# Items of 512 weight columns, taken in quarters of the contraction, in the first stage of a hybrid decoder block

## The chip, the core and the metric

The kernel runs on one core of a Trainium2 chip. The core has a matrix engine (TensorE, PE in the profile; its weight loads, which overlap, are listed as PEld), a vector engine (VectorE, DVE), an engine for activations and copies (ScalarE, ACT), a general engine (GpSimd, POOL), an engine that here only issues transfers (SyncE, SP), and 16 DMA engines. The engines run their own instruction queues in order and wait for one another by semaphores. The metric is the device time of one execution in microseconds; before the change the median of three runs is 1727.08 us (1726.94 to 1728.37).

## What is computed

One layer of a decoder block on 1024 tokens of 1024 features, all in float32. The part that matters here is the combined input projection and what takes its columns:

```
h = rms_norm(x, attn_norm_w)
proj = h @ w_in                       # columns: q 1024 | k 1024 | v 1024 | u 2048 | g 2048
q, k, v, u, g = split(proj)
q, k = rms_norm of each 64 columns of q and of k      # 8 heads of 2 x 64
a = diff_attention(q, k, v, lam, rel_bias)            # needs a bias row per head and distance
c = causal_depthwise_conv(u_a * sigmoid(u_b))         # width 31, over tokens
...
x = x + (sigmoid(g_a) * y_a + sigmoid(g_b) * y_b) @ w_out
x = x + (silu(h2 @ w_gate) * (h2 @ w_up)) @ w_down
```

## The kernel before

**Matrix products.** A float32 operand is split into a high part (a cast on ACT, `split_hi`, L120) and a low part (a subtraction, `split_lo` on DVE, L125, or `low` on POOL, L131, which of the two is set by `low_by_pool`). `mm3` (L168 to L170) issues three matmuls for a product: high by high, high by low, low by high. The normalized input stands in SBUF as `hT_hi` and `hT_lo`, 8 tiles of the contraction by 1024 tokens.

**The weight stream.** `Stream` holds a list of loads. `fetch` runs loads until more than `ahead` are ready; `next` hands out the oldest. A load takes a raw tile of 128 x 1024 (`wraw`, two buffers), issues the DMA on SP's queue, and splits it into `whi` and `wlo` (three buffers each, `wsplit`). `ld_wide` serves an item of 256 weight columns in two loads, each with half of the contraction (4 tiles of 128 rows by 256 columns).

**The first stage.** `opening` normalizes and transposes x, does V0 (v's first 256 columns) and half of U0. Then come the items of `first`, V1 and V2, each 256 columns of v; then seven u pairs (`u_pair`), which use seven products in place of eight and need sums of h (`sums_of_h`, on POOL) and of weights (`prepare`); then the items of `last`, Q0 (128 columns of q and 128 of k of the first head) and V3. After that the attention begins, with Q1 to Q7 and the g items as filling work between its steps.

`v_item` computes two token tiles of 128 x 256 into one PSUM bank (`gemm_N`: all 8 tiles of the contraction for one token tile, then the next), splits the bank into high and low, and sends both to DRAM by SP; it yields after each bank, four times. `q_item` does the same for the token half b = 1 and then b = 0, two banks each: ACT copies the bank and takes eight sums of squares, and after the second bank DVE forms 16 row factors and multiplies. The turning of q and k (`turn_qk`: transposes on PE, a scaled copy on ACT, the remainder on DVE, moves between partition halves by SP's DMAs) is put off by one yield through the list `late`.

**Banks.** In the first stage matrix products rotate over four PSUM banks (`pg`: two of tag pg, two of tag pg2). In the attention two are left, and the four banks of the convolution's accumulator and of pg2 serve the scores.

**Order.** The instructions are written in program order by these generators, and a scheduler then orders each engine's queue. At each yield of the first stage `bg.step` puts 3.25 steps of the depthwise convolution (taps on DVE, L594) into the program. `bg.until` after Q0 puts in all that is left for the first four channel tiles, whose accumulators lie in PSUM. At yields 18, 19 and 20 `bias_rows` makes a third of the bias rows: one-hot rows in and bias rows out by POOL's DMA queue, a matmul (L771) and a copy on ACT (L772) between.

Of the kernel before, what the change touches and what calls it, by code (L numbers as in the profile page):

```python
# [10 lines left out]
F32 = mybir.dt.float32  # L11
F32R = mybir.dt.float32r
AF = mybir.ActivationFunctionType
ALU = mybir.AluOpType
# [43 lines left out]
def kernel(  # L58
# [193 lines left out]
    def pcol(key, k=0):  # L252
        c = col[key] + k
        return pvec[:, c : c + 1]
# [63 lines left out]
    def ld_wide(w, cols):  # L318


        def half(g):
            def go():
                raw = wraw()
                r3 = raw[:].rearrange("p (k c) -> p k c", c=256)
                o = 0
                for c0, n in cols:
                    nc.sync.dma_start(
                        r3[:, :, o : o + n],
                        w[512 * g : 512 * (g + 1), c0 : c0 + n].rearrange(
                            "(k p) c -> p k c", p=P  # L330
                        ),
                    )
                    o += n
                hi, lo = wsplit(raw)
                return (
                    hi[:].rearrange("p (k c) -> p k c", c=256),
                    lo[:].rearrange("p (k c) -> p k c", c=256),
                )

            return go  # L340

        return [half(0), half(1)]

    class Stream:


# [52 lines left out]

    first = ["V1", "V2"]
    last = ["Q0", "V3"]
    later = [
        ["Q1", "G0", "G1"],
        ["Q2", "G2", "G3"],
# [21 lines left out]
    for c in range(NKT):  # L428
        ws.plan(ld_cols(wpa, c * P))
    for c in range(NKT):  # L430
# [331 lines left out]
    def bias_rows(c0):  # L762

        if c0 == 0:
            pool.memset(rb[:], -BIG)
            pool.dma_start(rb[:NB, :], rel_bias)
            dve.tensor_scalar(rb[:], rb[:], -1.0, None, op0=ALU.mult)
        oh, gr = half("u3")[: NB + 1, :384], half("u2")[:H, :384]
        pool.dma_start(oh, buckets[:, c0 : c0 + 384])
        o = pm()  # L770
        pe.matmul(o[:H, :384], rb[:], oh, start=True, stop=True)  # L771
        act.copy(gr, o[:H, :384])  # L772
        pool.dma_start(b_d[:, c0 : c0 + 384], gr)

    def bias_skew(h):
        pool.dma_start(t_d[h][:], b_d[h : h + 1, :].to_broadcast([P, TL]))
# [6 lines left out]
    T = {}  # L783
    late = []

    def q_item(h):
        halves = [ws.next(), ws.next()]
        t = {}
        T[h] = t
        for b in (1, 0):  # L790
            raw = qkp.tile([P, 4, 256], F32, tag="qkraw", name=nm("qkraw"), bufs=2)
            ss = sm.tile([P, 16], F32, tag="ss16", name=nm("ss16"))
            for i2 in range(2):
                o = pg()
                for e in range(2):
                    gemm_N(o[:, 256 * e : 256 * (e + 1)], halves, hT_hi, hT_lo, 4 * b + 2 * i2 + e)
                act.copy(raw[:, 2 * i2 : 2 * i2 + 2, :], o[:].rearrange("p (e c) -> p e c", c=256))
                jk = sm.tile([P, VD], F32, tag="jk", name=nm("jk"), bufs=1)[:, :HD]
                for g in range(8):
                    act.activation(  # L800
                        jk, o[:, g * HD : (g + 1) * HD], AF.Square, accum_out=ss[:, 8 * i2 + g : 8 * i2 + g + 1]
                    )
                if i2 == 0:
                    yield
            r = rstd_of(ss[:], 16, 1.0 / HD, fast=h > 0)
            r4 = raw[:].rearrange("p i (g d) -> p (i g) d", d=HD)
            dve.tensor_tensor(r4, r4, r.unsqueeze(2).to_broadcast([P, 16, HD]), op=ALU.mult)

            def turn_qk(z, key, b, raw):


                dma = nc.sync.dma_start
                pt = pm("pQ")
                for i in range(4):
                    pe.transpose(pt[:, i * P : (i + 1) * P], raw[:, i, z * P : (z + 1) * P], ident[:])  # L815
                w = pcol(key + "n")

                def part(j):
                    return qkp.tile([P, 512], F32R, tag=f"{key}s{j}", name=f"{key}s{j}_{h}_{b}", bufs=2 if key == "q" else 3)

                s1, s2 = part(1), part(2)
                act.activation(s1[:], pt[:], AF.Identity, scale=w)
                lo = part(3) if key == "q" else qkp.tile([P, 512], F32R, tag="klo", name=f"klo_{h}_{b}", bufs=1)
                dve.scalar_tensor_tensor(lo[:], pt[:], w, f32(s1[:]), op0=ALU.mult, op1=ALU.subtract)
                if key == "q":
                    dma(f32(s2[HD:, :]), f32(s1[HD:, :]))
                    lo2 = part(4)
                    for one, two in ((s1, s2), (lo, lo2)):
                        if one is lo:
                            dma(f32(two[HD:, :]), f32(one[HD:, :]))  # L830
                        dma(f32(two[:HD, :]), f32(one[HD:, :]))
                        dma(f32(one[HD:, :]), f32(one[:HD, :]))
                    t["q", b] = (s1, lo), (s2, lo2)
                else:
                    act.activation(s2[HD:, :], pt[HD:, :], AF.Identity, scale=w[HD:, :])
                    dma(f32(s2[:HD, :]), f32(lo[HD:, :]))
                    dma(f32(s1[HD:, :]), f32(lo[:HD, :]))
                    t["k", b] = s1, s2

            for z, key in ((1, "k"), (0, "q")):
                free = NT * (h - 1) + (0 if key == "k" and b else NT if key == "q" and not b else NT // 2)
                late.append((free if h else 0, lambda a_=(z, key, b, raw): turn_qk(*a_)))
            yield

    inatt = [False]
    MAKE = {"V": v_item, "U": u_item, "Q": q_item, "G": g_item}

    def run(items):  # L850
        for it in items:
# [177 lines left out]
    def first_stage():  # L1029


        nonlocal qkp
        tsum = sums_of_h()
        yield from opening()
        ups = [prepare(win, (U0 + D + c * P, U0 + c * P), st[0], 2, c == 1) for c in range(1, NKT)]

        def weights_ahead():
            yield
            ws.ahead = 1
            ws.fetch()  # L1040
# [36 lines left out]
        bg.until((NKT - CONV_PSUM) * (CW + 1) - 1)  # L1077
        yield from run(last[1:])

    def opening():  # L1080

# [1053 lines left out]
```

## Time and profile before

| what | value |
|---|---|
| median of three runs (lowest, highest) | 1727.08 us (1726.94, 1728.37) |
| profiled execution: span from its first to its last instruction | 1725.7 us |
| V1 and V2 | 65.3 to 112.0 us of the span |
| seven u pairs | 112.0 to 250.7 us |
| Q0 and V3 | 250.7 to 297.5 us |
| first scores of the attention | 306.8 us |

The profiled execution has only its span on record; the median of the runs is 1.4 us longer, which is what lies around the span. In the rows of the profile L12 is line 12 of the kernel, `out<-in` are the tiles written and read, `x3` a count, and what stands in brackets or behind a second bar is the time that the engine was idle just before and what ended it. A matmul's duration overlaps that of the next; the distance of two starts is what the engine needs for one.

### The profile page before, as it was taken

To read this page: it belongs to the slowest core of one execution; us is meant where nothing else is said; L and a number is where in the kernel's file an instruction comes from. 1 tells how busy PE (TensorE), PEld (TensorE's weight loads), DVE (VectorE), ACT (ScalarE), POOL (GpSimd) and SP (SyncE) were. 2 spreads that over 40 slices of the span, in tenths; PEclk is the share of its full clock that TensorE was granted. 3 is DMA by queue.
4 is the path that set the end of the run, shared out by engine and by line. 5 is a ranking of instruction groups with operands and counts; after the bars stand their busy time and mean duration, and the time that the engine had idled before them with its cause. 6 is when DMAs were issued, how large, how long until landed. Compare 5 with 4: busy or idle time off the path is not lost.

```text
span 1725.7 us, 25863 instructions
## 1 busy us (share of the span) xinstructions
PE 1714.6 (99%) x9243; PEld 1477.9 (86%) x9243; DVE 1275.4 (74%) x2128; ACT 862.5 (50%) x1958; POOL 219.1 (13%) x207
## 2 busy tenths in 40 slices
PE   9999999999999999999999999999999999999999
PEld 7997889998998998988788888888888888888887
DVE  7675889898988888878687769966676666575544
ACT  5333335767777776756556325633333333333332
POOL 3997851000000000000000000000000000000000
PEclk9999999999999999999999999999999999999999
DMA  6344445336345344343973683245455445598663
GB/s 208 116 126 132 131 151 154 104 109 171 104 127 147 115 125 138 101 136 130 333 238 118 200 296 119 74 135 164 147 170 170 154 141 164 175 355 285 217 215 130
DMA packets 261604, 281.64 MB, mean 163 GB/s; under 512 B 16546, under 2 KB 181986, under 8 KB 261475
## 3 DMA queue, kind: packets, MB, share of 16 engines
q1 hardware_dynamic: 254160, 267.71, 48.3%
q0 software_dynamic: 5680, 9.39, 2.6%
q10 hardware_dynamic: 1634, 2.89, 0.5%
q8 instruction: 73, 1.20, 0.3%
q14 instruction: 57, 0.46, 0.1%
HBM read 181.84 MB, written 85.50 MB: 155 GB/s over the span
## 4 chain that ended last, share of the span: by engine, by line
PE 92%; DMA 3%; DVE 2%; ACT 1%; issue 1%; POOL 0%; SPq 0%; DVEq 0%; POOLq 0%; ACTq 0%
PE acc L980 29%; PE acc L488 12%; PE pg L168 12%; PE pg L169 12%; PE pg L170 12%; PE wo L1850 3%; PE sc L1290 2%; PE sc L1289 2%; PE pT L1328 2%; PE pg L1106 1%; DVE acc L594 1%; PE pW L168 1%; PE pW L169 1%; PE pW L170 1%; PE pQ L815 1%
## 5 line engine op out<-in xcount | busy, mean ns | idle before, releaser
L594 DVE SCALAR_TENSOR_TENSOR acc<-u,cw,acc 128x1023 f32<-128x1023 f32 (+14 forms) x240 | 303.4, 1264 | 23.2 <-ACT acc L588 20.7
L170 PE MATMUL pg<-whi,hT_lo 128*128 128x256 f32 x704 | 200.2, 285 | 0.0
L168 PE MATMUL pg<-whi,hT_hi 128*128 128x256 f32 x704 | 199.7, 285 | 0.4 <-DVE v L125 0.4
L169 PE MATMUL pg<-wlo,hT_hi 128*128 128x256 f32 x704 | 199.5, 284 | 0.0
L125 DVE TENSOR_TENSOR wlo<-draw,whi 128x1024 fp32r<-128x1024 f32 x75 | 91.7, 1223 | 83.4 <-ACT whi L120 78.9
L120 ACT CAST whi<-draw 128x1024 fp32r<-128x1024 f32 x75 | 79.1, 1055 | 129.5 <-PE acc L488 114.3
L169 PEld LDWEIGHTS pg<-wlo,hT_hi 128*128 128x128 f32 x704 | 134.4, 191 | 1.8
L170 PEld LDWEIGHTS pg<-whi,hT_lo 128*128 128x128 f32 x704 | 134.3, 191 | 1.8
L168 PEld LDWEIGHTS pg<-whi,hT_hi 128*128 128x128 f32 x704 | 134.0, 191 | 2.1 <-DVE v L125 0.6
L120 ACT CAST whi<-wraw 128x1024 fp32r<-128x1024 f32 x90 | 94.7, 1052 | 70.6 <-PE pg L169 32.6
L488 PE MATMUL acc<-wlo,whi 128*128 128x512 f32 x308 | 119.8, 389 | 0.0
L488 PE MATMUL acc<-whi,wlo 128*128 128x512 f32 x308 | 119.8, 389 | 0.0
L1296 ACT ACTIVATE E<-E,mn 128x640 f32<-128x640 f32 (+7 forms) x128 | 99.8, 781 | 30.8 <-DVE mn L1291 29.2
L168 PE MATMUL pg<-hT_hi,whi 128*128 128x512 f32 x288 | 114.4, 397 | 0.1
L169 PE MATMUL pg<-hT_lo,whi 128*128 128x512 f32 x288 | 113.7, 395 | 0.0
L170 PE MATMUL pg<-hT_hi,wlo 128*128 128x512 f32 x288 | 113.7, 395 | 0.0
L120 ACT CAST whi<-s 128x1024 fp32r<-128x1024 f32 x54 | 56.9, 1053 | 104.9 <-PE acc L980 101.8
L125 DVE TENSOR_TENSOR wlo<-wraw,whi 128x1024 fp32r<-128x1024 f32 x75 | 93.3, 1246 | 12.6 <-ACT whi L120 12.3
L1291 DVE CUSTOM_DVE_ANT_0 E<-sc,tb 128x512 f32<-128x512 f32 (+3 forms) x128 | 74.2, 585 | 33.2 <-PE pT L1328 16.1
L980 PE MATMUL acc<-h_hi,whi 128*128 128x512 f32 x240 | 93.4, 389 | 0.0
L980 PE MATMUL acc<-h_lo,whi 128*128 128x512 f32 x240 | 93.4, 389 | 0.0
L980 PE MATMUL acc<-h_hi,wlo 128*128 128x512 f32 x240 | 90.1, 389 | 0.0
(370 smaller groups left out, 4589.7 us busy)
## 6 DMA issues: line engine op xcount, KB each, us to landing
wraw<-in_w_gate_up_dram SPq DMA_DIRECT2D x44, 512.0 KB, 4.7
wraw<-in_w_in_dram SPq DMA_DIRECT2D x38, 512.0 KB, 4.0
qs<-qs SPq DMA_DIRECT2D x96, 128.0 KB, 2.3
wd<-in_w_down_dram SPq DMA_DIRECT2D x44, 256.0 KB, 3.1
tdT<-wd SPq DMA_DIRECT2D x88, 128.0 KB, 4.8
draw<-sdS SPq DMA_DIRECT2D x44, 256.0 KB, 3.7
draw<-tdT SPq DMA_DIRECT2D x44, 256.0 KB, 3.7
wraw<-in_w_in_dram SPq DMA_DIRECT2D x32, 256.0 KB, 3.3
```

The lines of the kernel that those rows point to most:

```text
L120: act.copy(dst, src)
L125: last_lo[0] = dve.tensor_tensor(dst, src, f32(hi), op=ALU.subtract).ins
L168: pe.matmul(o, lh, rh, start=start, stop=False)
L169: pe.matmul(o, lh, rl, start=False, stop=False)
L170: last_mm[0] = pe.matmul(o, ll, rh, start=False, stop=stop).ins
L488: m = pe.matmul(o[s_][i][:], l_[:, ts], r_[:, 512:], start=start and j + y_ == 0, stop=j == n - 1 and y_ == 2, skip_group_check=not start,)
L594: dve.scalar_tensor_tensor(a_, us[c][:, : S - n], cw[:, c, t : t + 1], a_, op0=ALU.mult, op1=ALU.add)
L980: last_mm[0] = pe.matmul(o[:], a_[x_][:, k, :], b_[y_][:, k, :], start=start and k + x_ + y_ == 0, stop=k == 3 and x_ == 1, skip_group_che ...
L1289: pe.matmul(o[:, :w], qh[:, qs], k, start=True, stop=False)
L1291: dve.tensor_tensor_reduce(e[:, ks], o[:, :w], tb[:, S - nk + c0 : S - nk + c0 + w], 1.0, mn[:, j : j + 1] if c0 else 3.0e38, ALU.add, ALU ...
L1296: act.activation(e[:, :nk], e[:, :nk], AF.Exp, bias=mn[:, j : j + 1], scale=-1.0, accum_out=l[:, j : j + 1])
L1850: last_mm[0] = pe.matmul(o[s_][i][:], A[u_], B[v_], start=start and j + y_ == 0, stop=j == 3 and y_ == 2, skip_group_check=not start,).ins
```

## The change

V1 and V2 become one item W1 of 512 columns of v; Q0 and V3 become one item W0 of 512 columns (128 of q, 128 of k, 256 of v). A load (`ld_quarters`) brings a quarter of the contraction, 2 tiles of 128 rows by 512 columns, so a raw tile is as large as before. A wide item works on four token tiles at a time, each with a bank of its own: quarter 0 for all four tiles, then quarter 1, 2 and 3. The second block of four token tiles takes quarters 1, 2, 3 and then 0, which is loaded a second time.

```diff
+    def ld_quarters(w, cols):
+        def quarter(g):
+            def go():
+                raw = wraw()
+                r3 = raw[:].rearrange("p (k c) -> p k c", c=512)
+                o = 0
+                for c0, n in cols:
+                    nc.sync.dma_start(
+                        r3[:, :, o : o + n],
+                        w[256 * g : 256 * (g + 1), c0 : c0 + n].rearrange("(k p) c -> p k c", p=P),
+                    )
+                    o += n
+                hi, lo = wsplit(raw)
+                return g, [t_[:].rearrange("p (k c) -> p k c", c=512) for t_ in (hi, lo)]
+            return go
+        return [quarter(g) for g in (0, 1, 2, 3, 0)]
...
-    first = ["V1", "V2"]
-    last = ["Q0", "V3"]
+    first = ["W1"]
+    last = ["W0"]
...
+        if it[0] == "W":
+            cols = [(V0 + 256, 512)] if c else [(Q0, P), (K0, P), (V0 + 768, 256)]
+            return ld_quarters(win, cols)
...
-        pool.dma_start(oh, buckets[:, c0 : c0 + 384])
+        nc.sync.dma_start(oh, buckets[:, c0 : c0 + 384])
...
-        pool.dma_start(b_d[:, c0 : c0 + 384], gr)
+        nc.sync.dma_start(b_d[:, c0 : c0 + 384], gr)
...
+    def wide_item(c):
+        def v_parts(i, o, j, n):
+            vh, vl = [t_[:, :n] for t_ in v_tiles[0]()]
+            split_hi(vh, o)
+            split_lo(vl, o, vh)
+            for src, dst in ((vh, v_hi), (vl, v_lo)):
+                for e in range(n // 256):
+                    nc.sync.dma_start(dst[j + e][i * P : (i + 1) * P, :], f32(src[:, 256 * e : 256 * (e + 1)]))
+        w = []
+        for second, b in enumerate((0, 1) if c else (1, 0)):
+            banks = [pg() for i in range(4)]
+            if c == 0:
+                raw = qkp.tile([P, 4, 256], F32, tag="qkraw", name=nm("qkraw"), bufs=2)
+                ss = sm.tile([P, 16], F32, tag="ss16", name=nm("ss16"))
+            for n in range(4):
+                if second and n < 3:
+                    g, (hi, lo) = w[n + 1]
+                else:
+                    ws.ahead = 0 if n == 3 else 1
+                    w.append(ws.next())
+                    g, (hi, lo) = w[-1]
+                for i in range(4):
+                    ts = slice((4 * b + i) * P, (4 * b + i + 1) * P)
+                    o = banks[i]
+                    for k in range(2):
+                        mm3(
+                            o[:], hT_hi[:, 2 * g + k, ts], hT_lo[:, 2 * g + k, ts], hi[:, k, :], lo[:, k, :],
+                            n + k == 0, n == 3 and k == 1,
+                        )
+                    if n < 3:
+                        continue
+                    if c:
+                        v_parts(4 * b + i, o[:], 1, 512)
+                        continue
+                    act.copy(raw[:, i, :], o[:, :256])
+                    jk = sm.tile([P, VD], F32, tag="jk", name=nm("jk"), bufs=1)[:, :HD]
+                    for y in range(4):
+                        act.activation(
+                            jk, o[:, y * HD : (y + 1) * HD], AF.Square, accum_out=ss[:, 4 * i + y : 4 * i + y + 1]
+                        )
+                    v_parts(4 * b + i, o[:, 256:], 3, 256)
+                if second and n < 3:
+                    ws.ahead = 0 if c else n
+                    ws.fetch()
+                if n < 3:
+                    yield
+            if c == 0:
+                q_turns(0, b, raw, ss)
+            yield
```

`q_turns` is the second part of `q_item` (row factors, the multiplication, `turn_qk` and its entry in `late`), moved out unchanged so that `wide_item` can call it. A wide item yields eight times, as two narrow ones did. The rest sets where things happen: the switch of the low parts to POOL moves from the end of `opening` to yield 5 of W1, where the first u pair's weights are now prepared (yield 4 before), and `bg.until` comes after the first of W0's blocks.

```diff
         for n, _ in enumerate(run(first)):
             if n < 5:
                 tsum.pop(0)()
-            if n == 2:
-                ws.ahead = 1
-                ws.fetch()
-                ws.ahead = 0
-            if n == 4:
+            if n == 5:
+                low_by_pool[0] = True
                 next(ups[0])
                 A = next(ups[0])
-            if n == 5:
                 while tsum:
                     tsum.pop(0)()
...
         ws.ahead = 2
-        yield from run(last[:1])
-        bg.until((NKT - CONV_PSUM) * (CW + 1) - 1)
-        yield from run(last[1:])
+        for n, _ in enumerate(run(last)):
+            if n == 3:
+                bg.until((NKT - CONV_PSUM) * (CW + 1) - 1)
+            yield
...
         v_tiles[0] = tiles_from(st[0], ("p1", "u3"))
-        low_by_pool[0] = True
         ws.ahead = 0
         yield from u_half(0, uw, 1)
```

More of the change, by code (lines that the diff above doesn't have):

```diff
@@ L784, with q_turns, turn_qk, part @@
     late = []
+    def q_turns(h, b, raw, ss):
+        t = T.setdefault(h, {})
+        r = rstd_of(ss[:], 16, 1.0 / HD, fast=h > 0)
+        r4 = raw[:].rearrange("p i (g d) -> p (i g) d", d=HD)
+        dve.tensor_tensor(r4, r4, r.unsqueeze(2).to_broadcast([P, 16, HD]), op=ALU.mult)
+        def turn_qk(z, key, b, raw):
+            dma = nc.sync.dma_start
+            pt = pm("pQ")
+            for i in range(4):
+                pe.transpose(pt[:, i * P : (i + 1) * P], raw[:, i, z * P : (z + 1) * P], ident[:])
+            w = pcol(key + "n")
+            def part(j):
+                return qkp.tile([P, 512], F32R, tag=f"{key}s{j}", name=f"{key}s{j}_{h}_{b}", bufs=2 if key == "q" else 3)
+            s1, s2 = part(1), part(2)
+            act.activation(s1[:], pt[:], AF.Identity, scale=w)
+            lo = part(3) if key == "q" else qkp.tile([P, 512], F32R, tag="klo", name=f"klo_{h}_{b}", bufs=1)
+            dve.scalar_tensor_tensor(lo[:], pt[:], w, f32(s1[:]), op0=ALU.mult, op1=ALU.subtract)
+            if key == "q":
+                dma(f32(s2[HD:, :]), f32(s1[HD:, :]))
+                lo2 = part(4)
+                for one, two in ((s1, s2), (lo, lo2)):
+                    if one is lo:
+                        dma(f32(two[HD:, :]), f32(one[HD:, :]))
+                    dma(f32(two[:HD, :]), f32(one[HD:, :]))
+                    dma(f32(one[HD:, :]), f32(one[:HD, :]))
+                t["q", b] = (s1, lo), (s2, lo2)
+            else:
+                act.activation(s2[HD:, :], pt[HD:, :], AF.Identity, scale=w[HD:, :])
+                dma(f32(s2[:HD, :]), f32(lo[HD:, :]))
+                dma(f32(s1[HD:, :]), f32(lo[:HD, :]))
+                t["k", b] = s1, s2
+        for z, key in ((1, "k"), (0, "q")):
+            free = NT * (h - 1) + (0 if key == "k" and b else NT if key == "q" and not b else NT // 2)
+            late.append((free if h else 0, lambda a_=(z, key, b, raw): turn_qk(*a_)))
     def q_item(h):
         halves = [ws.next(), ws.next()]
-        t = {}
-        T[h] = t
         for b in (1, 0):
@@ L804, in q_item @@
                     yield
[L805 to L844, printed above, removed]
+            q_turns(h, b, raw, ss)
             yield
@@ L848 @@
     MAKE = {"V": v_item, "U": u_item, "Q": q_item, "G": g_item}
+    def wide_item(c):
[15 more added lines that the diff above has]
+                    g, (hi, lo) = w[n + 1]
+                else:
+                    ws.ahead = 0 if n == 3 else 1
+                    w.append(ws.next())
+                    g, (hi, lo) = w[-1]
+                for i in range(4):
+                    ts = slice((4 * b + i) * P, (4 * b + i + 1) * P)
[25 more added lines that the diff above has]
+            yield
+    MAKE["W"] = wide_item
     def run(items):
```

## The prediction

> **What bounds the kernel now.** I read the page first, then the busy time by stages, then the timeline of TensorE.
>
> ```profile
> span 1725.7 us, 25863 instructions
> ...
> PE 1714.6 (99%) x9243; PEld 1477.9 (86%) x9243; DVE 1275.4 (74%) x2128; ACT 862.5 (50%) x1958; POOL 219.1 (13%) x207
> ...
> PE 92%; DMA 3%; DVE 2%; ACT 1%; issue 1%; POOL 0%; SPq 0%; DVEq 0%; POOLq 0%; ACTq 0%
> ```
>
> TensorE (PE) is busy 99% of the span, and the chain that ended last runs over PE for 92%. The page warns that a busy PE need not be at its peak, so the stages that the change touches have to be seen alone: V1 with V2, the seven u pairs, Q0 with V3 (columns: busy time and count of PE, PEld, DVE, ACT, POOL, then the granted clock).
>
> ```profile
> 65.27:111.95 46.68, 46.68 (x388) 46.59 (x387) 31.70 (x30) 15.84 (x19) 44.26 (x22) 1.00 0.39 125
> 112.00:247.90 135.90, 135.80 (x601) 109.89 (x600) 103.41 (x97) 52.44 (x71) 102.78 (x67) 1.00 0.42 127
> 250.67:297.50 46.83, 46.83 (x393) 46.80 (x391) 44.58 (x50) 23.45 (x85) 9.37 (x9) 1.00 0.64 174
> ```
>
> All three run at the full clock with no idle PE to speak of. POOL is nearly full in the first (44.26 of 46.68 us), VectorE (DVE) in the last (44.58 of 46.83). What PE pays for one matmul there is the distance between starts, not the duration:
>
> ```profile
> 54.83 0.39 PE L170 MATMUL pg<-hT_hi,wlo 128*128 128x512 f32 x1
> ...
> 65.04 0.39 PE L170 MATMUL pg<-hT_hi,wlo 128*128 128x512 f32 x1
> 65.27 0.28 PE L168 MATMUL pg<-whi,hT_hi 128*128 128x256 f32 x1
> ...
> 72.46 0.28 PE L168 MATMUL pg<-whi,hT_hi 128*128 128x256 f32 x1
> ```
>
> From 54.83 to 65.04 there are 45 matmuls of 512 columns: 10.21 / 45 = 0.2269 us each. From 65.27 to 72.46 there are 60 of 256 columns: 7.19 / 60 = 0.1198 us. Twice 0.1198 is 0.2396, so a matmul has a fixed cost of 0.2396 - 0.2269 = 0.0127 us beside its columns. So **PE's own work is the bound**, and in these items half as many matmuls, twice as wide, pay it half as often.
>
> **The matmuls.** V1, V2, Q0 and V3 issue 192 each (8 token tiles, 8 contraction tiles, 3 products): 768 x 0.1198 = 92.0 us. W1 and W0 issue 192 each of 512 columns: 384 x 0.2269 = 87.1 us. **Term: -4.9 us**, 2.45 in each item. It reaches the end whole only if PE stays full, so the rest of this part asks what can make PE wait.
>
> [...]
>
> **Weights.** A quarter is one raw tile of 1024 columns, as a half was: a load, a cast on ACT, a subtraction. Each wide item takes five where two narrow ones took four.
>
> ```profile
> L120 ACT CAST whi<-wraw 128x1024 fp32r<-128x1024 f32 x90 | 94.7, 1052 | 70.6 <-PE pg L169 32.6
> ...
> L125 DVE TENSOR_TENSOR wlo<-wraw,whi 128x1024 fp32r<-128x1024 f32 x75 | 93.3, 1246 | 12.6 <-ACT whi L120 12.3
> ...
> wraw<-in_w_in_dram SPq DMA_DIRECT2D x38, 512.0 KB, 4.0
> ...
> L131 POOL TENSOR_TENSOR wlo<-wraw,whi 128x1024 fp32r<-128x1024 f32 x3 | 7.3, 2435 | 0.0
> ```
>
> A quarter lasts 24 x 0.2269 = 5.45 us on PE. There are three buffers of split weights, so quarter 3 can be split when quarter 0's matmuls end, 10.9 us before it is needed; the split takes 1.05 + 1.25 us (DVE in W1) or 1.05 + 2.44 us (POOL in W0). The repeated quarter 0 has the same 10.9 us. The 4.0 us load goes ahead into a raw tile. Hidden: 0. Since the switch to POOL moves to yield 5 of the W items, all five of W1's subtractions fall to DVE, three more than now, 3.7 us against 15.0 us idle in the first window; POOL loses two of 2.44 us, and the prepared weights of the first u pair come no later. Without that cover the first pair would wait; I keep 0 to +1.
>
> **The burst at a block's end.** A narrow item drained one bank per 5.75 us. A wide block finishes four banks within its last quarter, one per 6 x 0.2269 = 1.36 us, and the next block wants each 4.1 us after it was finished.
>
> ```profile
> L120 ACT CAST v<-pg 128x512 fp32r<-128x512 f32 x4 | 2.4, 589 | 6.2 <-PE pg L170 6.1
> L797 ACT COPY qkraw<-pg 128x512 f32<-128x512 f32 x4 | 2.3, 582 | 8.8 <-PE pg L170 8.8
> ...
> L125 DVE TENSOR_TENSOR v<-pg,v 128x512 fp32r<-128x512 f32 x4 | 2.7, 682 | 0.0
> ```
>
> ```profile
> 261.05 0.22 ACT L800 ACTIVATE jk<-pg 128x64 f32<-128x64 f32 x1
> 261.17 0.19 ACT L800 ACTIVATION_READ_ACCUMULATOR jk<-pg 128x1 f32 x1
> 261.39 0.22 ACT L800 ACTIVATE jk<-pg 128x64 f32<-128x64 f32 x1
> ```
>
> W1: cast and subtraction take 0.59 + 0.68 us per tile, in time. But the results leave through two buffers by SyncE (SP), four DMAs a tile instead of two:
>
> ```profile
> L746 SPq DMA_DIRECT2D v_hi<-p x7: 359/360/370, 73.3 to 108.4; - x7
> ...
> DMA to landing us min/median/max: 2.1/2.2/5.0
> ```
>
> 4 x 0.36 = 1.44 us of issue a tile, and the fourth tile waits for the second's landing: about the time at which its bank is wanted. **+0.2 us** (0 to +1.5).
>
> W0: a tile costs ACT a copy and a cast of 256 columns (0.35 each, an estimate from 0.58 at 512) and four squares at 0.34 us (261.05 to 261.39): 2.1 us against 1.36. The fourth bank is read by 1.36 + 8.4 = 9.8 us after the last quarter began, its subtraction 0.4 us later, and is wanted at 5.45 + 4.1 = 9.5: **+0.6 us**. A conv tap in front of the subtraction on DVE would make it 1.9 (0 to +2).
>
> **W0 to the attention.** One wait goes there and a like one comes:
>
> ```profile
> 298.04 0.39 PE L168 MATMUL pg<-whi,hT_hi 128*128 128x256 f32 x1 [0.36 <-DVE v L125]
> ```
>
> Here PE stood 0.36 us for a bank. After the change W0's second block ends in the same burst as its first, and the next item has only two banks: I take 0.7 for 0.36, **+0.3 us** (-0.4 to +2). The larger matter is the first head. Q0's q and k for tokens 0 to 511 are now complete when W0 ends, where V3 used to follow:
>
> ```profile
> 275.11 0.23 ACT L800 ACTIVATE jk<-pg 128x64 f32<-128x64 f32 x1
> ...
> 287.70 1.22 DVE L807 TENSOR_TENSOR qkraw<-qkraw,r 128x1024 f32<-128x1024 f32 x1
> ...
> 291.29 0.69 ACT L822 ACTIVATE ks<-pQ,pvec 128x512 fp32r<-128x512 f32 x1 [1.17 <-PE pQ L815]
> ...
> 302.97 1.01 ACT L598 COPY done<-acc 128x1024 f32<-128x1024 f32 x1 [3.76 <-DVE acc L594]
> ...
> 306.78 0.40 PE L1289 MATMUL sc<-ks,qs 128*128 128x512 f32 x1
> ```
>
> From the last square (275.3) to the first scores (306.8) lie 31 us, most of them conv taps that DVE put between the steps. After: W0 starts at 250.7 - 2.4 = 248.2 and ends at 248.2 + 43.6 + 0.6 = 292.4; ACT reads the last tile until 296.7. By then the taps, done at 302.97 with a stage that starts 2.4 us earlier, are nearly used up. What is left alone is some 2.2 us for the row factors (eight short steps), 1.2 for the multiplication, 1.0 for transposes, 1.4 for ks and klo, and a DMA of 0.5 + 2.3 us:
>
> ```profile
> qs<-qs SPq DMA_DIRECT2D x96, 128.0 KB, 2.3
> ```
>
> so scores at about 305.5 to 307, as now. Meanwhile PE has Q1's groups, 48 x 0.1198 = 5.75 us each. Two run at once in the two banks, until 292.7 + 11.5 = 304.2; the third needs ACT to have read the first (eight squares and a copy, 3.3 us). In time if ACT reads it before it turns to ks: **0** (0 to +13, below).
>
> **Bias rows.** Six DMAs go from POOL to SP.
>
> ```profile
> 143.11 0.39 PE L980 MATMUL acc<-hT_hi,wlo 128*128 128x512 f32 x1
> 143.60 0.50 PE L980 MATMUL acc<-hT_hi,whi 128*128 128x512 f32 x1
> ...
> L773 POOL DMA_DIRECT2D b_d<-u x3: 505/514/538, 138.4 to 150.5; - x3
> ```
>
> POOL gains 6 x 0.51 = 3.1 us where PE waits 143.60 - 143.11 - 0.23 = 0.26 us for weights. On SP, which is in order, a store now waits for ACT's copy of the row, and the next pair's loads and u's stores stand behind it for some 3 us; they are due a pair (19 us) ahead. **-0.1 us** (-0.3 to +1).
>
> **Sum.** -4.9 + 0.2 + 0.6 + 0.3 - 0.1 = -3.9, less than 0.1 us off for the W1 start: 1725.7 becomes 1721.8. The runs' median, 1727.08, stands 1.4 us over the profiled span, so **1723.1 us**. About 0.2% (3.5 us) is what a measurement of this kernel can tell from no change, and the forecast lies only just beyond it.
>
> **Rivals.**
> 1. *The bursts eat it.* For it: ACT's 2.1 against 1.36 us and a DVE that is full in the last window. W1's burst at its upper end (+1.5), W0's with a tap (+1.9) and 1.0 behind W0 make 4.4 in place of 1.1: -0.6, **1726.5 us**. Against it: the banks' 4.1 us of slack.
> 2. *The first head is late: slower.* Place: the two banks behind W0. If ACT takes ks ahead of Q1's first reading, and the row factors are threaded between taps as now (275.3 to 291.3 is 16 us), ks starts at 296.7 + 16 = 312.7, the first bank is free at 312.7 + 1.2 + 3.3 = 317.2, and PE stands from 304.2: 13.0 us, **1736 us**. Each us past 304.2 costs one; from 308.1 the kernel is slower than before, from 311.6 by over 0.2%. Against it: the taps have run out by about 300.
> 3. *The wide matmuls have no cheaper step*, so the change does not do what it says. Were a 512-column matmul twice a 256-column one, the term would be 0 and the waits +1.0: **1728.1 us**. Against it: the two distances quoted. [...]
>
> **How the numbers follow.** Forecast 0.60 (own range 1720 to 1724.5: the term whole, both small gains, minus a us of waits that reshuffle later; or a us more of bursts), rival 1 0.22, rival 2 0.15, rival 3 0.03. The range takes in all but rival 2's larger half and the forecast's tail: 1720 to 1730. Faster by over 0.2% (below 1723.6) 0.55, nearly all of the forecast; slower by over 0.2% (above 1730.5) 0.15, rival 2; within 0.2% 0.30.
>
> **What would show it.** Starts 0.227 us apart in both wide items, each 43.6 us long; PE gaps at W0's change of blocks of about 0.6 us with DVE's subtraction named; first scores 14 us after W0's last matmul, with two to three Q1 groups between them; no PE wait near 143. Wrong would be: a PE gap of several us between W0 and the first scores (rival 2), more than 2 us at the changes of blocks (rival 1), steps near 0.24 us (rival 3), or PE waiting for a quarter's weights, which I count at nothing.

## The result: slower by about 16 us

| kernel | median of the runs (lowest, highest) | span of the profiled execution |
|---|---|---|
| before | 1727.01 us (1726.01, 1728.37) | 1725.7 us |
| after | 1743.26 us (1741.58, 1743.94) | 1741.8 us |

The ratio of after to before is 1.0094, with a 95% interval of 1.0081 to 1.0107. The forecast was 1723.1 us with a range of 1720 to 1730: the sign was wrong, and the time lies outside the range. Below, "mended" kernels of the same change come out at 1724.7 to 1725.4 us, so nearly all of the loss is in what the change left around the two wide items and not in the items.

**The page of after.** Its span, its busy times and its chain:

```profile
span 1741.8 us, 25199 instructions
...
PE 1714.6 (98%) x8859; PEld 1460.1 (84%) x8859; DVE 1284.8 (74%) x2135; ACT 864.3 (50%) x1968; POOL 216.1 (12%) x200
...
PE 86%; DMA 5%; DVE 4%; ACT 2%; issue 1%; SPq 0%; POOL 0%; DVEq 0%; ACTq 0%
```

PE has 384 matmuls fewer, as the change says, and is busy for the same 1714.6 us. That is the trap of this line: a matmul that runs at half pace keeps PE busy for nearly twice as long (0.43 us from start to start at 846.57 us below, against 0.227), so a part of the loss hides in the busy time. The chain says more plainly that something else than PE now sets stretches of the time: PE's share falls from 92% to 86%, that of DMA rises from 3% to 5%, VectorE's from 2% to 4%.

**Stages of after** (columns as before: busy time and count of PE, PEld, DVE, ACT, POOL, then the granted clock, the share of DMA and GB/s):

```profile
66.09:110.20 44.11, 43.88 (x194) 35.99 (x194) 36.62 (x31) 16.22 (x20) 40.29 (x19) 1.00 0.36 120
110.20:252.90 142.70, 139.96 (x610) 112.90 (x609) 108.56 (x102) 55.15 (x74) 101.07 (x62) 1.00 0.44 139
...
840.30:845.50 5.20, 0.18 (x1) 0.00 (x0) 0.00 (x0) 3.45 (x6) 0.00 (x0) 0.73 1.05 405
845.50:849.00 3.50, 3.45 (x8) 2.80 (x9) 2.36 (x2) 0.95 (x1) 0.00 (x0) 0.50 1.05 398
```

The wide matmuls keep what was forecast of them: 43.88 us for 194 in W1's stretch is 0.226 us each. But the u pairs behind W1 lose 142.70 - 139.96 = 2.74 us that they did not lose before, and at 840 us, more than 500 us behind the last instruction of W0, PE stands for 5 us and then runs eight matmuls in 3.5 us, at half the clock.

**TensorE's waits in after**, from its timeline (start and duration; in brackets the idle time before and what ended it):

```profile
122.24 0.50 PE L1062 MATMUL acc<-hT_hi,whi 128*128 128x512 f32 x1 [1.03 <-ACT whi L120]
...
124.69 0.50 PE L1062 MATMUL acc<-hT_hi,wlo 128*128 128x512 f32 x1 [1.72 <-POOL wlo L131]
...
296.34 0.41 PE L168 MATMUL pg<-whi,hT_hi 128*128 128x256 f32 x1 [2.05 <-DVE v L125]
...
307.16 1.04 PE L823 MATMUL pQ<-ident,qkraw 128*128 128x128 f32 x8
...
315.34 0.40 PE L1367 MATMUL sc<-ks,qs 128*128 128x512 f32 x1
...
332.73 0.44 PE L1367 MATMUL sc<-ks,qs 128*128 128x384 f32 x1 [0.73 <-DVE mn L1369]
...
343.11 0.50 PE L1367 MATMUL sc<-ks,qs 128*128 128x512 f32 x1 [1.75 <-DVE mn L1369]
...
836.97 1.02 PE L168 MATMUL pg<-aTh,whi 128*128 128x512 f32 x2 [1.43 <-ACT aTh L120]
...
845.55 0.80 PE L168 MATMUL pg<-aTh,whi 128*128 128x512 f32 x1 [5.07 <-ACT whi L120]
...
846.57 0.63 PE L168 MATMUL pg<-aTh,whi 128*128 128x512 f32 x1
847.00 0.63 PE L169 MATMUL pg<-aTl,whi 128*128 128x512 f32 x1
```

Three places, and each becomes an experiment. **One**, the longest: 845.55, where `whi`, the high part of the attention projection's weights, is late. **Two**: 122.24 and 124.69, where the second u pair's weights are late. **Three**: 296.34 and what follows from W0's end, with the first scores at 315.34 instead of 306.78.

For the first place ScalarE's timeline tells why. Before (kept rows are the weight casts and the gates):

```profile
807.75 1.04 ACT L120 CAST whi<-wraw 128x1024 fp32r<-128x1024 f32 x1
...
824.62 1.05 ACT L120 CAST whi<-wraw 128x1024 fp32r<-128x1024 f32 x1
...
842.10 2.58 ACT L1633 ACTIVATE gt<-gt 128x512 f32<-128x512 f32 x4 [0.78 <-DMA gt<-g_d]
```

And after:

```profile
841.97 2.60 ACT L1711 ACTIVATE gt<-gt 128x512 f32<-128x512 f32 x4 [1.67 <-DMA gt<-g_d]
844.47 1.97 ACT L120 CAST whi<-wraw 128x1024 fp32r<-128x1024 f32 x2
```

Before, two weight tiles were cast at 807.75 and 824.62, ahead of the four gate activations; after, both come behind them, at 844.47, and the gates themselves wait for their transfer. The place in the code is this:

```python
    first_gates = last_of(mybir.EngineType.Activation)
    w3 = [ws.next()]
    with after(mean_hi), after(first_gates):
        w3.append(ws.next())
```

`next` first fetches until more than `ahead` loads are ready. With `ahead` at 2, the two tiles that this place needs were fetched by earlier calls, and what the constrained call splits is a tile that is wanted later. With `ahead` at 0 it splits the very tile that it hands out. (The code holds back only the second of the two tiles; in after the first one's cast stands behind the gates too, where ScalarE's queue has it.) Before, `ahead` is set to 2 ahead of Q0 and stays there; in the change W0's last quarter sets it with `ws.ahead = 0 if n == 3 else 1`, and nothing sets it back.

### The profile page after: what moved, and what is told of

Read it like the earlier page. It is cut to its first block, busy times and chain, and to the rows that moved or that the text cites. A ratio compares the mean times of both kernels' runs of the same rounds, so it can differ in the third digit from the quotient of the medians.

```text
span 1741.8 us, 25199 instructions
## 1 busy us (share of the span) xinstructions
PE 1714.6 (98%) x8859; PEld 1460.1 (84%) x8859; DVE 1284.8 (74%) x2135; ACT 864.3 (50%) x1968; POOL 216.1 (12%) x200
## 4 chain that ended last, share of the span: by engine, by line
PE 86%; DMA 5%; DVE 4%; ACT 2%; issue 1%; SPq 0%; POOL 0%; DVEq 0%; ACTq 0%
PE acc L1062 29%; PE acc L513 12%; PE pg L168 10%; PE pg L169 10%; PE pg L170 10%; PE wo L1928 3%; DVE acc L619 2%; PE sc L1368 2%; PE sc L1367 2%; PE pT L1406 2%; PE pg L1185 1%; PE pW L168 1%; PE pW L170 1%; PE pW L169 1%; DMA cT_lo<-lnd 1%
## 5 line engine op out<-in xcount | busy, mean ns | idle before, releaser
L619 DVE SCALAR_TENSOR_TENSOR acc<-u,cw,acc 128x1023 f32<-128x1023 f32 (+14 forms) x240 | 304.0, 1267 | 18.9 <-ACT acc L613 16.2
L168 PE MATMUL pg<-whi,hT_hi 128*128 128x256 f32 (+1 forms) x576 | 177.2, 309 | 2.3 <-DVE v L125 2.0
L169 PE MATMUL pg<-wlo,hT_hi 128*128 128x256 f32 (+1 forms) x576 | 178.0, 309 | 0.0
L170 PE MATMUL pg<-whi,hT_lo 128*128 128x256 f32 (+1 forms) x576 | 177.6, 309 | 0.0
L168 PEld LDWEIGHTS pg<-whi,hT_hi 128*128 128x128 f32 x576 | 109.9, 191 | 10.0 <-DVE v L125 2.5
L169 PEld LDWEIGHTS pg<-wlo,hT_hi 128*128 128x128 f32 x576 | 109.9, 191 | 6.7
L170 PEld LDWEIGHTS pg<-whi,hT_lo 128*128 128x128 f32 x576 | 110.0, 191 | 6.2
L125 DVE TENSOR_TENSOR wlo<-wraw,whi 128x1024 fp32r<-128x1024 f32 x78 | 100.8, 1294 | 18.3 <-ACT whi L120 17.5
```

What stands on the lines that cost most here:

```text
L125: last_lo[0] = dve.tensor_tensor(dst, src, f32(hi), op=ALU.subtract).ins
L168: pe.matmul(o, lh, rh, start=start, stop=False)
L169: pe.matmul(o, lh, rl, start=False, stop=False)
L170: last_mm[0] = pe.matmul(o, ll, rh, start=False, stop=stop).ins
L619: dve.scalar_tensor_tensor(a_, us[c][:, : S - n], cw[:, c, t : t + 1], a_, op0=ALU.mult, op1=ALU.add)
```

## The experiments

Each is timed against before on the same chip; ratios are to that. "e1" and so on are the labels.

**e1: after, with the lookahead put back.**

```diff
         for n, _ in enumerate(run(last)):
             if n == 3:
                 bg.until((NKT - CONV_PSUM) * (CW + 1) - 1)
             yield
+        ws.ahead = 2
```

> The changed kernel with one line more: the weight stream's lookahead is set to 2 again behind W0, where the change leaves it at 0. Theory A (the lookahead of 0, left over from W0's last quarter, lets the attention's filling work and the projection behind it fetch weights only when they are asked for): the waits at 825 to 850 us (some 13 us against some 2.5 before, the 5.24 us for a weight cast among them) go, time 1743.3 - 11 = 1732 us, give or take 1.5. Theory B (the first head's q and k are late, the attention's order is shifted and its end falls apart for that reason): the wait for a weight cast at the end of the attention stays, time 1743 us, give or take 2.

Measured: 1728.71 us (1726.12 to 1730.45), ratio 1.0012 [1.0003, 1.0021]. One line takes 14.5 of the 16.2 us away, some 2 us more than theory A's range allowed, and theory B is out. ScalarE in e1 has the order of before again:

```profile
810.28 1.05 ACT L120 CAST whi<-wraw 128x1024 fp32r<-128x1024 f32 x1 [0.53 <-PE pg L169]
...
824.55 1.04 ACT L120 CAST whi<-wraw 128x1024 fp32r<-128x1024 f32 x1
...
841.83 2.31 ACT L1711 ACTIVATE gt<-gt 128x512 f32<-128x512 f32 x4
```

and PE's only wait from 835 to 850 us is one of 0.46 us at 847.97. The 5.07 us at 845.55 are the largest part of the price and not all of it. The stretch from 800 to 1030 us in before, in after and in e1:

```profile
800.00:1030.00 230.00, 228.36 (x1039) 188.03 (x1038) 162.61 (x270) 113.18 (x198) 2.56 (x7) 1.00 0.67 226
...
800.00:1030.00 230.00, 219.83 (x989) 179.31 (x989) 150.49 (x251) 108.94 (x188) 2.54 (x7) 0.99 0.61 201
...
800.00:1030.00 230.00, 229.09 (x1051) 189.81 (x1051) 161.12 (x268) 114.15 (x199) 2.54 (x7) 1.00 0.67 227
```

PE is idle there for 1.6 us in before, 10.2 in after and 0.9 in e1, and it gets 62 matmuls less far in after than in e1.

**e2: before, with the lookahead taken away**, and no wide item at all.

```diff
         yield from run(last[1:])
+        ws.ahead = 0
```

> The kernel before with one line more: the lookahead is set to 0 behind V3, nothing else. Theory A: it alone makes the waits at the end of the attention, time 1727 + 11 = 1738 us, give or take 2. Theory B: 1727 us, give or take 2, since q and k are as early as before.

Measured: 1739.17 us (1738.71 to 1740.23), ratio 1.0074 [1.0059, 1.0089]: 12.5 us slower by this line alone (before on that chip: 1726.68). That is within theory A's range. ScalarE and then PE in e2:

```profile
839.27 2.61 ACT L1633 ACTIVATE gt<-gt 128x512 f32<-128x512 f32 x4 [4.79 <-DMA gt<-g_d]
841.78 1.97 ACT L120 CAST whi<-wraw 128x1024 fp32r<-128x1024 f32 x2
```

```profile
842.87 0.80 PE L168 MATMUL pg<-aTh,whi 128*128 128x512 f32 x1 [6.71 <-ACT whi L120]
```

The same order as in after, and the same wait, here 6.71 us long. With e1 and e2 the first place is shown from both sides: it is the lookahead that W0 leaves behind, worth 12.5 to 14.5 us.

**e3: W1 alone** (`first = ["W1"]`, `last = ["Q0", "V3"]`, bias rows by SyncE as in the change; the lookahead stays as before).

> W1 in place of V1 and V2, bias rows by SyncE, Q0 and V3 as before (and so a lookahead of 2). Theory A says that W1's 32 stores, bunched at the ends of its two blocks, hold the second u pair's weight load back on SyncE's queue (issued at 117.3 us in place of 108.9), which costs 3.1 us of PE at 122 to 125 us and eats W1's gain of 2.45: 1727.5 us, give or take 1. The rival (that wait comes from the bias rows or elsewhere, W1 gives its 2.45 us): 1724.6 us.

Measured: 1727.89 us (1725.38 to 1729.62), ratio 1.0005 [0.9996, 1.0015]. The median is in the first theory's range: W1's 2.45 us do not arrive. PE's waits in e3's u pair, and its windows around them:

```profile
121.55 0.50 PE L1062 MATMUL acc<-hT_hi,whi 128*128 128x512 f32 x1 [0.93 <-ACT whi L120]
...
123.99 0.80 PE L1062 MATMUL acc<-hT_hi,wlo 128*128 128x512 f32 x1 [1.71 <-POOL wlo L131]
```

```profile
121.00:124.00 3.00, 0.74 (x3) 0.31 (x3) 2.93 (x3) 2.08 (x4) 2.43 (x2) 0.99 0.15 47
124.00:127.50 3.50, 3.50 (x9) 2.79 (x10) 0.01 (x1) 1.01 (x1) 3.50 (x3) 0.52 0.00 0
127.50:131.00 3.50, 3.50 (x17) 2.90 (x16) 0.07 (x1) 1.05 (x1) 3.42 (x4) 1.00 0.55 136
```

The two waits cost 2.6 us, and behind them 9 matmuls, 2.0 us at full pace, take 3.5: another 1.5 us or so, at a granted clock of 0.52. SyncE's queue shows who stands in front of the late loads:

```profile
113.21 0.91 SPq L886 DMA_DIRECT2D v_hi<-p  x2
114.22 2.42 SPq L886 DMA_DIRECT2D v_lo<-u  x2
116.73 1.06 SPq L1026 DMA_DIRECT2D wraw<-in_w_in_dram  x2
```

L886 is W1's stores, four for each tile; L1026 is the second u pair's loads. Before, the two loads were issued at 108.86 and 110.08 us, each behind a single store. One more wait of e3 has no like in before: 1.26 us at 314.92, for ScalarE's squares; e6 and e9 come back to it.

**e4: W0 alone** (`first = ["V1", "V2"]`, `last = ["W0"]`, `ws.ahead = 2` behind it, bias rows by SyncE).

> V1 and V2 as before, W0 in place of Q0 and V3, lookahead set to 2 behind it, bias rows by SyncE. If the waits at 296 us (2.05 us for a bank) and at 333 and 343 us (2.5 us for DVE's minimum) belong to W0's own order, they stay: 1727 - 2.45 + 1.7 + 2.5 = 1728.8 us, give or take 1. If they come from the lookahead they go: 1724.5 us.

Measured: 1727.15 us (1726.01 to 1730.18), ratio 1.0006 [0.9996, 1.0015]. The third place is there without W1:

```profile
295.33 0.53 PE L168 MATMUL pg<-whi,hT_hi 128*128 128x256 f32 x1 [2.05 <-DVE v L125]
```

and the waits of 0.73 and 1.75 us for DVE's `mn` are there too, at 331.74 and 342.13. They belong to W0's own order, not to the lookahead. The time is below what was expected with these waits (1727.8 to 1729.8), so they cost the end less than they cost PE; and this kernel also has the bias rows on SyncE, which e6 takes alone. What e4 shows is that W0's gain of 2.45 us does not arrive.

**e5: e3, with the second u pair's two loads issued from ScalarE's queue** instead of behind the stores on SyncE.

```diff
-            nc.sync.dma_start(
+            queue.dma_start(
                 raw[:].rearrange("p (k c) -> p k c", c=P), w[:, c0 : c0 + P].rearrange("(k p) c -> p k c", p=P)
             )
...
-        ups = [prepare(win, (U0 + D + c * P, U0 + c * P), st[0], 2, c == 1) for c in range(1, NKT)]
+        ups = [prepare(win, (U0 + D + c * P, U0 + c * P), st[0], 2, c == 1, nc.scalar if c == 2 else nc.sync) for c in range(1, NKT)]
```

> W1 alone (e3), and the second u pair's two weight loads issued from ScalarE's queue instead of behind W1's 16 stores on SyncE; nothing else differs from e3 (1727.89 us, whose waits at 121.55 and 123.99 us sum to 3.0 us, with some 3.5 us at half pace behind them in the profiled execution). Theory A (the stores in front of the loads on SyncE make both waits): the loads are issued at about 113.5 us instead of 116.7, whi's cast ends by 118.5, both waits go and the half pace with them: 1723.0 to 1725.0 us. Rival B (the second pair is held by the high casts and POOL's low splits anyway, or ScalarE pays for the issues): the waits only move, 1727.0 to 1728.5 us.

Measured: 1726.24 us (1723.98 to 1730.87), ratio 0.9996 [0.9987, 1.0005]; e3 was at 1.0005 [0.9996, 1.0015]. The two intervals overlap, so here the profile has to carry it. The loads in e5 (count, shortest, median and longest, then first and last start), and PE's only wait of that stretch:

```profile
L1026 ACTq DMA_DIRECT2D wraw<-in_w_in_dram x2: 386/390/393, 108.2 to 110.8; - x2
```

```profile
118.99 0.50 PE L1062 MATMUL acc<-T2h,whi 128*128 128x512 f32 x1 [1.12 <-ACT p L1080]
```

Issued at 108.2 and 110.8 instead of 116.73, the loads are in time and both waits are gone, the half pace with them. A smaller one has come in their place: `p` of the u pair uses the buffer of W1's last high part and waits for its store. So the theory holds for the two waits, and a part of its rival for the size; the median lies between their two ranges. (This execution is 3 us over e5's median; it waits another 0.78 and 1.26 us at the first scores, at 310 and 312 us, like e6 below.)

**e6: before, with the bias rows by SyncE alone.**

```diff
-        pool.dma_start(oh, buckets[:, c0 : c0 + 384])
+        nc.sync.dma_start(oh, buckets[:, c0 : c0 + 384])
...
-        pool.dma_start(b_d[:, c0 : c0 + 384], gr)
+        nc.sync.dma_start(b_d[:, c0 : c0 + 384], gr)
```

> Before with one part of the change alone, the bias rows' two transfers issued by SyncE instead of GpSimd. Theory A (no path to the end runs through them, as the prediction's -0.1 says): 1726.4 to 1727.3 us. Rival B (GpSimd's issues delayed its low splits, the gain of this part is real): under 1726.0 us. Rival C (SyncE's queue, in order, makes weight loads behind them late): over 1727.7 us.

Measured: 1728.16 us (1726.00 to 1729.98), ratio 1.0009 [1.0000, 1.0018]. The time falls in rival C's range, but not by its mechanism: PE waits for no late weights at 140 us. It waits at the first scores, 170 us later:

```profile
312.36 0.50 PE L1289 MATMUL sc<-ks,qs 128*128 128x512 f32 x1 [1.79 <-DVE mn L1291]
...
314.36 0.58 PE L168 MATMUL pg<-whi,hT_hi 128*128 128x256 f32 x1 [1.26 <-ACT jk L800]
```

```profile
310.62 1.28 DVE L594 SCALAR_TENSOR_TENSOR acc<-u,cw,acc 128x1023 f32<-128x1023 f32 x1 [2.62 <-ACT acc L588]
311.82 0.48 DVE L1291 CUSTOM_DVE_ANT_0 E<-sc,tb,mn 128x256 f32<-128x256 f32 x1
```

In e6 the scores start 4 us sooner than in before, and a conv tap that waits for its accumulator then stands on DVE in front of a score's reduction. The six transfers themselves lie some 170 us ahead of that stretch. What differs there is the order: each engine's order of work is made anew when the kernel is built, and in this kernel VectorE does ten steps of the score reductions ahead of that tap where before it did six. That the order is the cause is read from the timelines and was not tested by itself; e9 bears on it. The profiled execution is 1.2 us over e6's median, so the two waits are the upper end of what this costs.

**e7: e4, with v's parts made ahead of the squares**, the squares read from the copy in SBUF, so that W0's banks are free sooner.

```diff
                     act.copy(raw[:, i, :], o[:, :256])
+                    v_parts(4 * b + i, o[:, 256:], 3, 256)
...
-                            jk, o[:, y * HD : (y + 1) * HD], AF.Square, accum_out=ss[:, 4 * i + y : 4 * i + y + 1]
+                            jk, raw[:, i, y * HD : (y + 1) * HD], AF.Square, accum_out=ss[:, 4 * i + y : 4 * i + y + 1]
                         )
-                    v_parts(4 * b + i, o[:, 256:], 3, 256)
```

> W0 alone (e4, 1727.15 us) with v's parts of a tile made ahead of the sums of squares, and these read from the copy in SBUF instead of the bank, so that the bank is free some 1 us of ScalarE's work sooner. Theory A (PE's 2.2 us at 295.3 and the half pace behind it come from ScalarE's order of reading W0's last tiles, and what PE wins there is kept): the wait falls under 0.7 us, Q1 starts by 294 us, the transposes and the scores come 1.5 to 3 us sooner, 1724.0 to 1725.7 us. Rival B (the first head's scores run on a chain of their own, statistics to scores, which sets the end of this stretch): the wait at 295.3 falls as well, but those at 331.7 and 342.1 us (0.90 and 1.92) grow by as much, 1726.5 to 1727.5 us.

Measured: 1728.84 us (1727.90 to 1732.15), ratio 1.0012 [1.0004, 1.0021]. A miss for both theories. The wait did not shrink but grew:

```profile
295.59 0.58 PE L168 MATMUL pg<-whi,hT_hi 128*128 128x256 f32 x1 [2.92 <-DVE v L125]
```

DVE here does five conv taps in a row until 292.3 us and only then the remainder of the first head's k, for which ScalarE stands 2.16 us, ahead of its copy of the third tile. In e4 the same five taps stand in the same place and end at 290.9, and ScalarE has no such wait. DVE comes to them 1.4 us later in e7; one step of the first block's row factors (L681) took 2.13 us in this execution where it took 0.17 in e4. W0's last matmul starts 0.6 us sooner (292.28 against 292.89), Q1's first 0.26 us later. So e7 does not tell whether ScalarE's reading of the banks is what holds PE at W0's end. In e4 the subtraction that releases PE starts at 294.85, when two things have just ended, ScalarE's cast and a tap on DVE; either would hold it without the other.

**e8: after, with all three mends** (e1's line, e5's queue, e7's order).

> The changed kernel with all three mends: the lookahead set to 2 behind W0 (e1, 1728.7 us), the second u pair's loads from ScalarE's queue, W0's banks released first. Theory A (the three causes are separate and sum up): e1's losses of 3.0 us at 121 to 124 and of 1.5 to 3 us at 296 go, 1722.0 to 1724.5 us. Rival B (what is won in W1 or W0 is lost again in the first head's scores): 1725.0 to 1728.0 us.

Measured: 1727.45 us (1726.42 to 1729.32), ratio 1.0002 [0.9994, 1.0011]: within rival B's range, but e7's edit is in it, which cost 1.7 us beside e4 by the medians.

**e9: e5 with the bias rows back on GpSimd's queue; e11: e1 likewise; e12: e11 with e5's queue.** These cross the loads' queue with the bias rows' queue.

> e5 (W1 alone, the second u pair's loads from ScalarE's queue, 1726.24 us, 0.9996 of before) with the bias rows' transfers back on GpSimd's queue; VectorE's order of work around the first scores is the same in both. Theory A (the bias rows' queue costs nothing by itself; the 1.4 us that the bias part cost before alone came from the order of work that was built anew with it): the same as e5, 1725.5 to 1727.0 us. Rival B (the queue itself costs 1 to 1.5 us): 1724.5 to 1725.3 us.

> e1 (the changed kernel with the lookahead set to 2 behind W0, 1728.7 us, 1.0012 of before) with the bias rows' transfers back on GpSimd's queue, so both W items without the third part of the change. Theory A (the queue costs nothing by itself): 1727.9 to 1729.2 us. Rival B (the queue itself costs 1 to 1.5 us): 1727.0 to 1727.7 us.

> e11 with the second u pair's two loads from ScalarE's queue, as in e5: the changed kernel's two items with the two mends that the runs bear out. Theory A (the loads' mend is worth the same 1.6 us here as between e3 and e5): 1726.5 to 1727.5 us, no better than before, since W0's own waits (2.2, 0.9 and 1.9 us) stay. Rival B (PE's gain in the u pair is lost in the first head's scores): 1728 to 1729 us.

Measured: e9 1725.46 us (1723.53 to 1727.96), ratio 0.9993 [0.9984, 1.0001], not to be told from e5, and between its two ranges. Its execution has e6's two waits as well, 0.51 us at 308.75 and 1.26 at 310.74, with the bias rows on GpSimd; so these waits do not need SyncE's queue, which fits the order as their cause. e11 1730.25 us (1728.39 to 1733.08), ratio 1.0021 [1.0011, 1.0030], slower than either theory allowed, a miss. e12 1724.74 us (1724.33 to 1725.97), ratio 0.9991 [0.9982, 1.0000], faster than either, another. The row that explains e11 is a new wait of PE, with GpSimd's timeline beside it:

```profile
139.37 0.80 PE L796 MATMUL pm<-u,rb 33*8 33x384 f32 x2 [1.82 <-DMA u<-in_buckets_dram]
```

```profile
129.95 4.75 POOL L131 TENSOR_TENSOR wlo<-s,whi 128x1024 fp32r<-128x1024 f32 x2
...
137.21 0.53 POOL L794 DMA_DIRECT2D u<-in_buckets_dram  x1
```

GpSimd makes the low parts of the late weights, is late with them, and issues the one-hot rows of the bias only behind them; the bias matmul then holds PE. (This execution, 1733.08 us, is the slowest of e11's.) With the loads in time (e12) there is no such wait. So e12's mend takes the waits for the late weights (0.29 and 1.71 us in this execution) and the one for the bias away at once, 5.5 us beside e11 by the medians.

**e13: e12 with the bias rows on SyncE, as the change has them.**

> The changed kernel with the lookahead set to 2 behind W0 and the second u pair's loads from ScalarE's queue, the bias rows left on SyncE as the change has them: the fourth corner beside e1 (1728.7 us), e11 (1730.3) and e12 (1724.7). Theory A (in e11 the bias rows on GpSimd cost 2.0 us only because the late loads made its queue late; with the loads in time the queue of the bias rows is worth nothing): as e12, 1724.2 to 1725.5 us. Rival B (bias rows by SyncE are worth 1.5 us in any case): 1722.7 to 1723.7 us. Rival C (they cost 1.4 us, as before alone in e6): 1725.7 to 1727 us.

Measured: 1725.39 us (1724.18 to 1731.05), ratio 0.9990 [0.9981, 1.0000]. The median is in theory A's range, and rival B's is outside the interval; rival C's (1725.7 to 1727) is not, so a cost of a microsecond is not excluded. The four corners are:

| medians, us | bias rows by SyncE | bias rows by GpSimd |
|---|---|---|
| u pair's loads behind W1's stores | e1 1728.7 | e11 1730.3 |
| u pair's loads from ScalarE's queue | e13 1725.4 | e12 1724.7 |

e12 and e13 are the two wide items without the loss: some 2 us faster than before by their medians, at the edge of what their intervals can tell from it, and 18 us faster than the change as it was made. W0's waits are still in both; in e12 the wait at W0's end is

```profile
293.23 0.39 PE L168 MATMUL pg<-whi,hT_hi 128*128 128x256 f32 x1 [2.05 <-DVE v L125]
```

## Why the prediction was wrong

- **The matmuls, -4.9 us: right.** Steps of 0.226 us in W1 and 0.227 in W0, 384 matmuls fewer. Rival 3 is out.
- **Weights, "Hidden: 0": this is the step that failed.** For the quarters themselves it held: PE waits for none of them. But it priced only the five loads of each item, and a weight stream has a state that outlives the item. The lookahead after W0's last quarter is 0 where it was 2, and the consumer that pays stands 550 us later. Price: 12.5 us (e2) to 14.5 us (e1) in place of 0. The line was in the diff; asking which value the next reader finds would have been enough to see it, and the four lines of `w3` would have told what a call with lookahead 0 holds back. Of the 20 us between the forecast and the result this step is 14.5 (after to e1), the second u pair's loads 3.3 (e1 to e13), and W0's waits with all the rest 2.3 (e13 to 1723.1), by medians from different chips.
- **"The prepared weights of the first u pair come no later": right, and the wrong pair.** It is the second pair whose loads come 8 us later, at 116.7 (e3) instead of 108.9.
- **The burst at a block's end, +0.2 us for W1.** At W1's change of blocks the wait was 0.4 us from start to start (88.27 us in after), near the forecast. I worked out 1.44 us of store issue a tile, and asked only what it does to the banks, not what stands behind sixteen stores in SyncE's queue. Price in e3: 2.6 us of waits, and in some executions 1.5 us of half pace; with the bias rows on GpSimd 2 us more (e11).
- **W0's burst, +0.6 us:** no wait at the change of blocks.
- **W0 to the attention, +0.3 us: too small.** The wait is 2.05 us instead of 0.36, the first matmuls behind it run at half pace for 3.2 us, and two waits of 0.73 and 1.75 us follow at the first head's scores. I had ScalarE done with the last tile at 296.7; it was done at 300.6, since W0 ended 1.7 us later than I had it and a weight cast of 1.07 us and a copy of the accumulator of 1.04 us came in between. That the row factors and the multiplication would then stand alone for some 3 us was right. The scores started at 315.3 instead of 305.5 to 307, with the transposes on PE behind Q1's matmuls, 21 us behind W0's last matmul and not 14. In sum W0's gain of 2.45 us is used up (e4: 1.0006). This was rival 2's place but not its mechanism: PE never stood for a third Q1 group, it ran from 296.34 to the first scores without a wait. The price on PE's timeline was some 5.6 us (1.7 + 1.4 + 0.7 + 1.8) in place of 13, and e4's time, 0.5 us over before, says that more than 2 us of it do not reach the end; where they are made up was not followed. Why PE waits just there is not settled, since e7 missed.
- **Bias rows, -0.1 us.** By the medians they cost 1.4 us alone, with a rebuilt order (e6, at the edge of its interval); with the late loads they saved 1.5 (e11 against e1, whose intervals overlap); with the loads in time nothing that can be measured (e13 against e12). The runs give this part no fixed price.
- **The chances.** Slower by over 0.2% had 0.15, all of it on the first head. No rival held a place outside the stages that the change touches.

## What to carry to other kernels

When an edit sets a value that others read (a lookahead, a buffer's owner, which engine makes the low parts), write down the value that it leaves behind and go to the next reader, however far. For each burst of transfers on a queue, name the next load behind it and its due time (behind W1's stores the second u pair's loads were issued 8 us late, at 116.73 us in e3). And where the order of work is built anew with each edit, an edit of no cost may move 1 to 2 us elsewhere (e6, at the edge of its interval): measure it alone, and read a small gain from the waits that go, not from the median.

## What the hardware showed that was not expected

**A stall can cost more than its length.** After PE's 2.05 us at W0's end the granted clock is 0.53 for 3.2 us, in after:

```profile
294.10:296.30 2.20, 0.20 (x1) 0.00 (x0) 2.19 (x4) 2.17 (x11) 0.00 (x0) 1.00 1.06 322
...
296.40:299.60 3.20, 3.20 (x16) 3.20 (x17) 1.65 (x2) 3.11 (x15) 0.00 (x0) 0.53 0.99 237
299.80:303.00 3.20, 3.20 (x28) 3.20 (x28) 2.39 (x8) 1.00 (x7) 0.00 (x0) 0.97 0.99 344
```

16 matmuls instead of 28 in the same 3.2 us. So a stall of 2 us was followed by a loss of some 1.4 us more, and one of 5 us (845.55) by eight matmuls in 3.5 us, 0.43 us apart (846.57 to 847.00). It is not in each execution: in after the waits of 1.03 and 1.72 us at 122 and 124 us were followed by the full pace, the like waits of e3 by half pace.

Where the half clock begins bears on this. In after the granted clock is 0.50 three times: from 296.57 to 299.98 us, from 842.70 to 849.52 and from 1740.40 to the end of the trace. The first stretch lasts 3.41 us and the second twice that, and the two later starts lie 160 and 423 times 3.413 us behind the first. Cut into pieces of that length (in e3 from the start of its half clock, 123.97), PE's busy time around the two waits is, in after and then in e3:

```profile
119.07:122.48 3.41, 2.38 (x11) 1.69 (x10) 3.30 (x4) 1.04 (x1) 0.21 (x1) 1.00 0.98 298
122.48:125.89 3.41, 1.70 (x7) 1.08 (x7) 2.06 (x2) 2.61 (x4) 3.41 (x3) 1.00 0.00 0
...
120.56:123.97 3.41, 0.79 (x3) 0.30 (x2) 3.34 (x3) 2.52 (x4) 2.40 (x2) 1.00 0.28 86
123.97:127.38 3.41, 3.39 (x8) 2.72 (x9) 0.04 (x1) 1.01 (x1) 3.41 (x3) 0.50 0.00 0
```

In after a border falls between the two waits, in e3 both lie in one piece. In after, from 20 us on, half clock followed the three pieces at full clock in which PE was busy, by the profile, for 0.90, 1.20 and 1.37 us of 3.41, and none of those with 1.66 us or more; in e3 it followed the one with 0.79. In e6 it began at about 313.0 us, behind a piece with some 1.6 us (an estimate from its granted clock of 0.57 between 312.36 and 317.00 us and its wait of 1.79 us). So the like waits cost their length in after and some 1.5 us more in e3, and what the traces show to differ is where they fall among these pieces.
